# Joining 256-column projections into 512-column products with tokens on the partitions

## The chip, the cores and the metric

The kernel runs on one core of a Trainium2 chip. The metric is the device time of one execution in microseconds; "before" is the median of three executions on the chip. A profile is one further execution, recorded by the hardware profiler.

## What is computed

One block of a hybrid encoder for 256 tokens of width 2048, everything in float32. The input is normalised (u), one projection `w_in` gives the inputs of two mixers, and their outputs go through `w_out`; a SwiGLU FFN and a last normalisation follow. Cut to what the change touches:

```python
u = rms_norm(h, norm1_g[l])
P = u @ w_in[l]
z, xbc, dt_raw, pr = P[..., :o1], P[..., o1:o2], P[..., o2:o3], P[..., o3:]
prev = jnp.pad(pr, ((0, 0), (1, 0), (0, 0)))[:, :-1]
pr = pr + (prev - pr) * rwkv_mu[l]                 # token shift; r, k, v are slices of pr
xbc = jax.nn.silu(causal_depthwise_conv(xbc, conv_w, conv_b))   # x, B, C are slices of xbc
y_ssd = ssd_mixer(...)                             # chunked state space mixer, 4 groups
y_rwkv = rwkv7_mixer(...)                          # 32 heads, recurrence over the tokens
h = h + jnp.concatenate([y_ssd, y_rwkv], axis=-1) @ w_out[l]
v = rms_norm(h, norm2_g[l])
h = h + (jax.nn.silu(v @ w_gate[l]) * (v @ w_up[l])) @ w_down[l]
return rms_norm(h, norm_f_g)
```

## The kernel before

**Products in three parts.** Every large product is done in float32 accuracy with three matmuls: each operand is split into a rounded part and a rest (`uh`, `ul` for the activations, `whi`, `wlo` for the weights), and hi x hi, hi x lo and lo x hi are summed. The weights arrive by DMAs of SyncE's queue (SP) in units of 128 x 1024 elements in a ring of four `raw` buffers; ScalarE writes `whi` (L192), VectorE `wlo` (L193), each in a ring of four.

**Two forms of a product.** `gemm_a` (L267) makes 256 output columns with the weights stationary: 96 matmuls whose moving side is the 256 tokens. The result has channels on the partitions and tokens along the row. As the normalisation factor belongs to a token, VectorE multiplies the result in PSUM by a broadcast row `R` (`scaled`, L229). `gemm_b` (L284) makes 512 output columns with the activations stationary: 96 matmuls of 512 columns; the result has tokens on the partitions, so the factor can be a per-partition scale. Both keep their results in the pool `mm` of four PSUM tiles; `gemm_a` uses one tile, `gemm_b` two. A second PSUM pool, `mx`, also of four, serves all the small work.

**The order of the work.** A `Side` object holds small functions with due times. `gemm_a` advances its clock by half a tick after every two of its 16 k tiles (four ticks a product), `gemm_b` by half a tick after every k tile (eight ticks for 16). Functions whose time has come are traced there, between the product's matmuls; `drain` traces all that is left. This order is the priority by which the instructions are then laid out on each engine.

**RWKV.** There are eight pairs of two 128-channel blocks. Window `pi` (loop at L908) multiplies k, v and r of pair `pi`, 256 columns each, with the token shift (`shift`, L359: one ScalarE and one VectorE instruction a block) behind each product. From window 4 on, two output products of four k tiles (`out_rwkv`, L900) follow the values. So windows 0 to 3 have 12 ticks, windows 4 to 7 have 16. In them, `window` (L882) places three stages of side work: `PREP` for pair `pi`, `AMATS` and `INV` (the matrices and their inverse) for pair `pi - 1`, and `CHAIN` (four state steps, group norm, `final` with the output parts `yh`, `yl`) for pair `pi - 2`. With 16 ticks or more, the times hold as written, with 12 they are compressed.

**State space mixer.** After window 7, `window(8, 20)` and two output products, four 256-column products give B and C with their convolution (`conv`, L928: one ScalarE and three VectorE instructions a block) and one silu over all of `BC`. Then, for each of four groups, two 256-column products give x, convolved at once; output products of finished work and the 512-column product for z follow, with the previous group's side work (`SSD` times) in their ticks.

The FFN (L1116) uses 512-column products throughout; its gated values are turned by eight PE transposes (`back`, L1103), which are due 1.5 ticks after the up product.

Of the kernel before, what the change touches and what calls it, by code (L numbers as in the profile page):

```python
# [10 lines left out]
F32 = mybir.dt.float32  # L11
F32R = mybir.dt.float32r
AF = mybir.ActivationFunctionType
# [3 lines left out]
P = 128  # L17
T = 256
D = 2048
KT = D // P  # L20
D_FF = 5632
CXBC = 2048
CDT = 5120
CR = 5152
CK = 7200
CV = 9248
# [4 lines left out]

PREP = (1.081, 1.2, 4.2, 5.2, 5.536, 6.756, 8.05, 9.2)
AMATS = (0.132, 1.4, 2.027, 2.231, 2.69, 3.323, 6.493)
INV = (4.9, 5.9, 6.9, 8.4, 10.4, 11.4, 12.9, 14.9)
STEPS = (0.667, 2.0, 5.0)
# [31 lines left out]
def tile_hybrid_block(ctx: ExitStack, tc: tile.TileContext, x, norm1_g, w_in, conv_w, conv_b, dt_bias, A_log, D_skip,  # L69
                      ssd_norm_g, mu, w0, w2, a0, a2, g2, k_k, k_a, r_k, gn_w, gn_b, w_out, norm2_g, w_gate, w_up,  # L70
                      w_down, norm_f_g, out):
    nc = tc.nc
    PS = bass.MemoryType.PSUM
    x = x[0]
    out = out[0]
    w_in, conv_w, w2, a2, g2 = w_in[0], conv_w[0], w2[0], a2[0], g2[0]
# [4 lines left out]
    wpool = ctx.enter_context(tc.tile_pool(name="wpool", bufs=3))  # L81
# [4 lines left out]
    side = Side()  # L86
# [4 lines left out]
    def mxt(name):  # L91
        return mx.tile([P, 512], F32, name=name, tag="mx")
# [7 lines left out]
    ident = const.tile([P, P], F32, name="ident")  # L100
# [13 lines left out]
    ps = mxt("ps_up")  # L114
# [9 lines left out]
    rows = [init.tile([P, P], F32, name=f"rows{i}") for i in range(3)]  # L124
# [13 lines left out]
    MU, W0, A0, KK, KA, RK = 0, 48, 64, 80, 96, 112  # L138
# [13 lines left out]
    for hh in range(2):  # L152
        for s in range(2):
            m = mask2[hh * 64:(hh + 1) * 64, s]
# [4 lines left out]
    for s in range(2):  # L159
        for hh in range(2):  # L160
            a = hh * 64
# [20 lines left out]
    ps = mxt("ps_cols")  # L182
    nc.tensor.transpose(out=ps[:, :16], in_=rown, identity=ident[:16, :16])
    tc.keep_in_program_order(nc.vector.tensor_copy(colN, ps[:, :16]))
    colA = const.tile([P, P], F32, name="colA")
# [10 lines left out]
    uh = ul = R = None  # L196
    ssq = [const.tile([P, 2, 4], F32, name=f"ssq{i}") for i in range(3)]
    rstd = [const.tile([P, 2], F32, name=f"rstd{i}") for i in range(3)]
# [30 lines left out]
    def scaled(ps):  # L229

        nc.vector.tensor_tensor(ps, ps, R.unsqueeze(1).broadcast_to([P, 2, T]), ALU.mult)
        return ps
# [34 lines left out]
    def gemm_a(w, cols, name, units=None):  # L267
        ps = mmt(name)
        for k0 in range(0, KT, 4):
            hi, lo = split(load_a(w, cols, k0)) if units is None else units(k0 // 4)  # L270
            for k in range(4):
                kt = k0 + k
                first, last = kt == 0, kt == KT - 1
                for b in range(2):
                    o = ps[:, b]
                    wh, wl = hi[:, k, b * P:(b + 1) * P], lo[:, k, b * P:(b + 1) * P]
                    nc.tensor.matmul(o, wh, uh[:, kt], start=first and b == 0, stop=False)  # L277
                    nc.tensor.matmul(o, wh, ul[:, kt], start=False, stop=False)  # L278
                    nc.tensor.matmul(o, wl, uh[:, kt], start=False, stop=last and b == 1)  # L279
                if k % 2:  # L280
                    side.tick(0.5)
        return ps

    def gemm_b(w, r0, c0, acts, name, turned=False):  # L284


        ps = [mmt(name).rearrange("p a t -> p (a t)") for _ in range(2)]
        n = len(acts)
        wv = w[r0:r0 + n * P, c0:c0 + 512].rearrange("(k p) c -> p k c", p=P)
        for k0 in range(0, n, 2):  # L290
            raw = wpool.tile([P, 2, 512], F32, name="raw", tag="raw", bufs=4)
            if turned:
                nc.sync.dma_start(out=raw[:, 0], in_=wv[:, k0])
                for a in range(2):
                    nc.sync.dma_start(out=raw[a * 64:a * 64 + 64, 1], in_=wv[64 - a * 64:P - a * 64, k0 + 1])
            else:
                nc.sync.dma_start(out=raw, in_=wv[:, k0:k0 + 2])
            hi, lo = split(raw)
            for k in range(2):
                kt = k0 + k  # L300
                first, last = kt == 0, kt == n - 1
                ah, al = acts[kt]
                for b in range(2):
                    s = slice(b * P, (b + 1) * P)
                    nc.tensor.matmul(ps[b], ah[:, s], hi[:, k], start=first, stop=False)  # L305
                    nc.tensor.matmul(ps[b], ah[:, s], lo[:, k], start=False, stop=False)  # L306
                    nc.tensor.matmul(ps[b], al[:, s], hi[:, k], start=False, stop=last)  # L307
                side.tick(0.5)
        return ps

    def add_out(w, r0, ys, then=None, turned=False, ns=range(4)):

# [30 lines left out]
    for r, c in ((rows[1], colB), (rows[0], colA), (rows[2], colC)):  # L343
        ps = mxt("ps_cols")
# [4 lines left out]
    omA = const.tile([P, 48], F32, name="omA")  # L349
# [9 lines left out]
    def shift(dst, ps, om, m):  # L359
        nc.scalar.activation(dst, ps, AF.Copy, scale=om)  # L360
        nc.vector.scalar_tensor_tensor(dst[:, 1:], ps[:, :T - 1], m, dst[:, 1:], ALU.mult, ALU.add)
# [10 lines left out]
    pst = ExitStack()  # L372
    pp = pst.enter_context(tc.tile_pool(name="pp", bufs=1, side="right"))
# [508 lines left out]
    def window(pi, ticks):  # L882
        if pi < 8:
            w = pairs[pi]
            w["load"]()
            for t, n in zip(PREP, ("decay", "rate", "keys", "keys2", "keysum", "btt", "vt", "ktt")):
                side.at(t, w[n])
        if 0 < pi < 9:
            w = pairs[pi - 1]
            for t, f in zip(AMATS, w["amats"]):  # L890
                side.at(t, f)
            for t, f in zip(INV, w["inv"]):
                side.at(t if ticks >= 16 else t * (ticks - 0.5) / 16, f)
        if pi > 1:
            for t, f in zip(CHAIN, pairs[pi - 2]["chain"]):
                side.at(t if ticks >= 16 else t * (ticks - 0.5) / 16, f)
# [3 lines left out]
    def out_rwkv(q, ns):  # L900

        if q < 0:
            return
        if ns[0] == 0:
            held[:] = [yq.popleft(), yq.popleft()]
        add_out(w_out, 2048 + q * 512, held, turned=True, ns=ns)

    for pi in range(8):  # L908
        st = {}
        pairs.append(rwkv_pair(pi, st))  # L910
        window(pi, 16 if pi > 3 else 12)
        for i, (n, c) in enumerate((("k", CK), ("v", CV), ("r", CR))):
            ps = scaled(gemm_a(w_in, [(0, 256, c + pi * 256)], "ps_rkv"))
            t = pp.tile([P, 2, T], F32, name="rkv", tag="t" + n, bufs=1)
            for j in range(2):
                m = ((c - CR) // P) + 2 * pi + j
                shift(t[:, j], ps[:, j], omA[:, m:m + 1], colA[:, MU + m:MU + m + 1])
            st[n] = t
            if n == "v":
                out_rwkv(pi // 2 - 2, (2 * (pi % 2), 2 * (pi % 2) + 1))  # L920
        side.drain()


# [4 lines left out]
    def conv(dst, ps, blk):  # L928
        w = [colC[:, 24 * j + blk:24 * j + blk + 1] for j in range(4)]
        nc.scalar.activation(dst, ps, AF.Identity, bias=colB[:, CB + blk:CB + blk + 1], scale=w[3])  # L930
        for s in range(1, 4):
            nc.vector.scalar_tensor_tensor(dst[:, s:], ps[:, :T - s], w[3 - s], dst[:, s:], ALU.mult, ALU.add)

    for i in range(4):
        ps = scaled(gemm_a(w_in, [(0, 256, CXBC + 2048 + i * 256)], "ps_bc"))
        if i == 0:
            pst.close()
            bcp = xzst.enter_context(tc.tile_pool(name="bcp", bufs=1, side="right"))
            xz = xzst.enter_context(tc.tile_pool(name="xz", bufs=2, side="right"))
            BC = bcp.tile([P, 2, 4, T], F32, name="BC")  # L940
        for j in range(2):
            b = 2 * i + j
            conv(BC[:, b // 4, b % 4], ps[:, j], 16 + b)
    nc.scalar.activation(BC, BC, AF.Silu)
    side.drain()
    window(9, 18)

    def ssd_group(g, xc, zs):
        st = {}
# [104 lines left out]
    for g in range(4):  # L1054
        xc = []
        if g == 0:
            out_rwkv(2, (2, 3))
        elif g == 1:
            out_rwkv(3, (0, 1, 2, 3))
        for i in range(2):  # L1060
            ps = scaled(gemm_a(w_in, [(0, 256, CXBC + g * 512 + i * 256)], "ps_xs"))
            t = xz.tile([P, 2, T], F32, name="xc", tag=f"xc{i}")
            for j in range(2):
                conv(t[:, j], ps[:, j], 4 * g + 2 * i + j)
            nc.scalar.activation(t, t, AF.Silu)
            xc.append(t)
        if g >= 2:
            add_out(w_out, (g - 2) * 512, [yq.popleft() for _ in range(2)])
        psz = gemm_b(w_in, 0, g * 512, uacts, "ps_z")
        zs = xz.tile([P, 2, 512], F32, name="zs")  # L1070
        for b in range(2):
            nc.scalar.activation(zs[:, b], psz[b], AF.Silu, scale=rstd[0][:, b:b + 1])
        side.drain()
        if g == 0:
            est.close()
            est = ExitStack()
            sp = est.enter_context(tc.tile_pool(name="sp", bufs=1))
        for t, f in zip(SSD, ssd_group(g, xc, zs)):
            side.at(t if g < 3 else t / 3, f)
# [119 lines left out]
```

## Time and profile before

| | |
|---|---|
| Median of 3 executions | 1674.48 us (1671.82 to 1675.09) |
| Profiled execution | 1671.13 us |
| Its span | 1669.4 us, mean clock of TensorE 0.996 |
| DMA traffic | 286.97 MB, mean 172 GB/s |

The stages of the profiled execution, by the first matmuls of the products:

| Stage | us from the span's start |
|---|---|
| RWKV windows 0, 1, 2, 3 | 38.1, 76.6, 117.8, 185.9 |
| RWKV windows 4, 5, 6, 7 | 242.2, 309.0, 376.5, 443.7 |
| Two output products, B and C | 510.6 |
| State space groups and their output products | 585.8 |
| FFN | 930.6 to the end |

In the profile's lines, "L279 PE MATMUL ps_rkv<-uh,wlo" is a matmul of TensorE made by line 279 that writes the tile `ps_rkv`. PEld are the weight loads of TensorE, which overlap its matmuls; DVE is VectorE, ACT ScalarE, SPq the queue that issues DMAs. A line of groups ends with the busy time in us, the mean length of one in ns, and the engine's idle time before them with what ended it. Records of matmuls overlap, since they are pipelined: the time of a product is read from first start to first start.

### The profile page before, as it was taken

How to read it: one execution, taken by the hardware profiler on the slowest of the kernel's cores; microseconds unless marked ns; L12 is line 12 of the kernel's file. 1: busy time of each engine (PE TensorE's matmuls, PEld its weight loads, DVE VectorE, ACT ScalarE, POOL GpSimd, SP SyncE). 2: the span in 40 equal slices, each digit the busy share in tenths (PEclk: the TensorE clock that was granted, in tenths of full speed). 3: DMA queues.
4: the chain of work that ended last, by engine and by line, in shares of the span. 5: the costliest groups of instructions: out<-in, count | busy, mean ns of one | idle time of the engine just before them, and what ended most of it. 6: DMA issues, size and time to landing. Idle time of an engine off the chain costs nothing.

```text
span 1669.4 us, 31147 instructions
## 1 busy us (share of the span) xinstructions
PE 1640.1 (98%) x12514; PEld 1422.7 (85%) x12514; DVE 1172.9 (70%) x1827; ACT 910.7 (55%) x1488; POOL 17.9 (1%) x57
## 2 busy tenths in 40 slices
PE   8999999999999999999999999999999999999997
PEld 8998898988888988998988888888888888888886
DVE  7887898788887867877778656465565564554657
ACT  6654775766755648657665544444444444444444
POOL 3000000000000000000000000000000000000000
PEclk9998999999999999999999999999999999999999
DMA  8653554454455556765655666666666666666663
GB/s 247 184 143 104 134 135 126 137 140 139 138 142 144 154 152 188 233 191 155 180 176 152 202 189 190 194 189 189 196 190 189 190 189 196 189 191 192 190 189 126
DMA packets 219473, 286.97 MB, mean 172 GB/s; under 512 B 41762, under 2 KB 124480, under 8 KB 218688
## 3 DMA queue, kind: packets, MB, share of 16 engines
q1 hardware_dynamic: 218000, 282.68, 58.1%
q8 instruction: 98, 1.61, 0.4%
q0 software_dynamic: 752, 1.24, 0.3%
q10 hardware_dynamic: 576, 1.05, 0.2%
q14 instruction: 47, 0.39, 0.1%
HBM read 281.75 MB, written 3.18 MB: 171 GB/s over the span
## 4 chain that ended last, share of the span: by engine, by line
PE 77%; DVE 9%; ACT 6%; issue 3%; DMA 3%; SPq 1%; DVEq 0%; POOL 0%; ACTq 0%
PE ps_o L305 8%; PE ps_o L306 8%; PE ps_o L307 8%; PE ps_gt L306 5%; PE ps_up L307 5%; PE ps_gt L305 5%; PE ps_up L306 5%; PE ps_gt L307 5%; PE ps_up L305 5%; DVE wlo L193 2%; PE ps_xs L277 2%; ACT whi L192 2%; PE ps_rkv L277 2%; PE ps_xs L278 2%; PE ps_xs L279 2%
## 5 line engine op out<-in xcount | busy, mean ns | idle before, releaser
L193 DVE TENSOR_TENSOR wlo<-raw,whi 128x1024 fp32r<-128x1024 f32 x508 | 619.9, 1222 | 376.9 <-ACT whi L192 375.8
L192 ACT CAST whi<-raw 128x1024 fp32r<-128x1024 f32 x508 | 532.7, 1051 | 596.8 <-PE ps_o L307 159.6
L277 PE MATMUL ps_rkv<-uh,whi 128*128 128x256 f32 x768 | 227.7, 296 | 0.0
L279 PE MATMUL ps_rkv<-uh,wlo 128*128 128x256 f32 x768 | 218.9, 285 | 0.0
L278 PE MATMUL ps_rkv<-ul,whi 128*128 128x256 f32 x768 | 218.8, 285 | 0.0
L277 PEld LDWEIGHTS ps_rkv<-uh,whi 128*128 128x128 f32 x768 | 147.5, 192 | 5.3 <-issue 0.7
L278 PEld LDWEIGHTS ps_rkv<-ul,whi 128*128 128x128 f32 x768 | 147.9, 193 | 1.2 <-issue 0.3
L279 PEld LDWEIGHTS ps_rkv<-uh,wlo 128*128 128x128 f32 x768 | 147.6, 192 | 0.4
L305 PE MATMUL ps_gt<-whi,uh 128*128 128x512 f32 x352 | 137.1, 389 | 0.0
L307 PE MATMUL ps_gt<-whi,ul 128*128 128x512 f32 x352 | 137.0, 389 | 0.0
L306 PE MATMUL ps_gt<-wlo,uh 128*128 128x512 f32 x352 | 136.9, 389 | 0.0
L305 PE MATMUL ps_up<-whi,uh 128*128 128x512 f32 x352 | 136.9, 389 | 0.0
L306 PE MATMUL ps_up<-wlo,uh 128*128 128x512 f32 x352 | 136.9, 389 | 0.0
L307 PE MATMUL ps_up<-whi,ul 128*128 128x512 f32 x352 | 136.9, 389 | 0.0
L305 PE MATMUL ps_o<-whi,ah 128*128 128x512 f32 x336 | 131.7, 392 | 0.0
L307 PE MATMUL ps_o<-whi,al 128*128 128x512 f32 x336 | 130.9, 390 | 0.0
L306 PE MATMUL ps_o<-wlo,ah 128*128 128x512 f32 x336 | 130.7, 389 | 0.0
L305 PE MATMUL ps_o<-whi,yh 128*128 128x512 f32 x256 | 105.6, 412 | 0.0
L307 PE MATMUL ps_o<-whi,yl 128*128 128x512 f32 x256 | 100.9, 394 | 0.0
L306 PE MATMUL ps_o<-wlo,yh 128*128 128x512 f32 x256 | 100.8, 394 | 0.0
L318 DVE TENSOR_TENSOR h<-ps_o,h 128x512 f32<-128x512 f32 x152 | 98.5, 682 | 1.7 <-PE ps_o L307 1.1
L306 PEld LDWEIGHTS ps_up<-wlo,uh 128*128 128x128 f32 x352 | 66.1, 188 | 13.7
(342 smaller groups left out, 2982.4 us busy)
## 6 DMA issues: line engine op xcount, KB each, us to landing
raw<-in_w_in_dram SPq DMA_DIRECT2D x180, 512.0 KB, 4.0
raw<-in_w_gate_dram SPq DMA_DIRECT2D x88, 512.0 KB, 3.7
raw<-in_w_up_dram SPq DMA_DIRECT2D x88, 512.0 KB, 3.7
raw<-in_w_down_dram SPq DMA_DIRECT2D x88, 512.0 KB, 4.6
raw<-in_w_out_dram SPq DMA_DIRECT2D x32, 512.0 KB, 4.0
raw<-in_w_out_dram SPq DMA_DIRECT2D x32, 256.0 KB, 4.2
raw<-in_w_out_dram SPq DMA_DIRECT2D x64, 128.0 KB, 4.0
csb<-cs_d SPq DMA_DIRECT2D x4, 1024.0 KB, 6.5
```

What stands on the lines that cost most here:

```text
L192: order(nc.scalar.copy(hi, raw))
L193: order(nc.vector.tensor_tensor(lo, raw, hi.bitcast(F32), ALU.subtract))
L277: nc.tensor.matmul(o, wh, uh[:, kt], start=first and b == 0, stop=False)
L278: nc.tensor.matmul(o, wh, ul[:, kt], start=False, stop=False)
L279: nc.tensor.matmul(o, wl, uh[:, kt], start=False, stop=last and b == 1)
L305: nc.tensor.matmul(ps[b], ah[:, s], hi[:, k], start=first, stop=False)
L306: nc.tensor.matmul(ps[b], ah[:, s], lo[:, k], start=False, stop=False)
L307: nc.tensor.matmul(ps[b], al[:, s], hi[:, k], start=False, stop=last)
L318: nc.vector.tensor_tensor(d, ps[b], d, ALU.add)
```

## The change

Thirteen pairs of 256-column products become 512-column products through a new function `rows_of`:

- the values of pair `pi` with the keys of pair `pi + 1` (`pi` 0 to 6), from two ranges of weight columns, which `gemm_b` now takes as a tuple and loads by two DMAs a unit; the keys of pair 0 get a product of their own ahead of window 0, and the values of pair 7 keep theirs in window 7
- B, and C
- x of each of the four groups

`rows_of` copies the two PSUM tiles to SBUF on ScalarE with the token's factor as scale, into a tile of the `raw` ring, and returns a function that turns 256 channels by four PE transposes into one `mx` tile. Token shifts and convolutions read that tile; they are side work now, due one tick after the product (1.5 for the second half of x). The silu over `BC` is done in two halves. The receptance r stays as it was. Two due times in `PREP` change: `vt` from 8.05 to 9.6, `ktt` from 9.2 to 8.05.

```diff
-PREP = (1.081, 1.2, 4.2, 5.2, 5.536, 6.756, 8.05, 9.2)
+PREP = (1.081, 1.2, 4.2, 5.2, 5.536, 6.756, 9.6, 8.05)
...
-        wv = w[r0:r0 + n * P, c0:c0 + 512].rearrange("(k p) c -> p k c", p=P)
+        parts = [(0, 256, c0[0]), (256, 256, c0[1])] if isinstance(c0, tuple) else [(0, 512, c0)]
+        wv = w[r0:r0 + n * P].rearrange("(k p) c -> p k c", p=P)
...
-                nc.sync.dma_start(out=raw, in_=wv[:, k0:k0 + 2])
+                for at, m, c in parts:
+                    nc.sync.dma_start(out=raw[:, :, at:at + m], in_=wv[:, k0:k0 + 2, c:c + m])
...
+    def rows_of(c0, name):
+
+
+        ps = gemm_b(w_in, 0, c0, [(uh[:, k], ul[:, k]) for k in range(KT)], name)
+        rows = wpool.tile([P, 2, 512], F32, name="rows_in", tag="raw", bufs=4)
+        for b in range(2):
+            nc.scalar.activation(rows[:, b], ps[b], AF.Copy, scale=rstd[0][:, b:b + 1])
+
+        def channels(i):
+            ps = mxt("ps_tr").rearrange("p (j t) -> p j t", j=2)
+            for j in range(2):
+                for b in range(2):
+                    c = i * 256 + j * P
+                    nc.tensor.transpose(out=ps[:, j, b * P:(b + 1) * P], in_=rows[:, b, c:c + P], identity=ident)
+            return ps
+
+        return channels
...
+    def channels_of(st, n, pi, ps):
+        t = pp.tile([P, 2, T], F32, name="rkv", tag="t" + n, bufs=1)
+        for j in range(2):
+            m = (dict(k=CK, v=CV, r=CR)[n] - CR) // P + 2 * pi + j
+            shift(t[:, j], ps[:, j], omA[:, m:m + 1], colA[:, MU + m:MU + m + 1])
+        st[n] = t
+
+    sts = [{} for _ in range(8)]
+    channels_of(sts[0], "k", 0, scaled(gemm_a(w_in, [(0, 256, CK)], "ps_rkv")))
     for pi in range(8):
-        st = {}
+        st = sts[pi]
         pairs.append(rwkv_pair(pi, st))
         window(pi, 16 if pi > 3 else 12)
...
+        if pi < 7:
+
+            turn_to = rows_of((CV + pi * 256, CK + (pi + 1) * 256), "ps_vk")
+            side.at(1, lambda f=turn_to, st=st, pi=pi: channels_of(st, "v", pi, f(0)))
+            side.at(1, lambda f=turn_to, st=sts[pi + 1], pi=pi: channels_of(st, "k", pi + 1, f(1)))
+        else:
+            channels_of(st, "v", pi, scaled(gemm_a(w_in, [(0, 256, CV + pi * 256)], "ps_rkv")))
+        out_rwkv(pi // 2 - 2, (2 * (pi % 2), 2 * (pi % 2) + 1))
+        channels_of(st, "r", pi, scaled(gemm_a(w_in, [(0, 256, CR + pi * 256)], "ps_rkv")))
         side.drain()
...
-        ps = scaled(gemm_a(w_in, [(0, 256, CXBC + 2048 + i * 256)], "ps_bc"))
...
-    nc.scalar.activation(BC, BC, AF.Silu)
+    def conv_bc(f, i):
+        for m in range(2):
+            ps = f(m)
+            for j in range(2):
+                b = 2 * m + j
+                conv(BC[:, i, b], ps[:, j], 16 + 4 * i + b)
+        nc.scalar.activation(BC[:, i], BC[:, i], AF.Silu)
+
+    turn_b = rows_of(CXBC + 2048, "ps_bc")
...
+    side.at(1, lambda: conv_bc(turn_b, 0))
+    turn_c = rows_of(CXBC + 2560, "ps_bc")
     side.drain()
     window(9, 18)
+    side.at(1, lambda: conv_bc(turn_c, 1))
...
-        for i in range(2):
-            ps = scaled(gemm_a(w_in, [(0, 256, CXBC + g * 512 + i * 256)], "ps_xs"))
+        turn_x = rows_of(CXBC + g * 512, "ps_xs")
+
+        def conv_x(i, f=turn_x, g=g, xc=xc):
             t = xz.tile([P, 2, T], F32, name="xc", tag=f"xc{i}")
+            ps = f(i)
             for j in range(2):
                 conv(t[:, j], ps[:, j], 4 * g + 2 * i + j)
             nc.scalar.activation(t, t, AF.Silu)
             xc.append(t)
+
+        side.at(1, lambda f=conv_x: f(0))
+        side.at(1.5, lambda f=conv_x: f(1))
```

More of the change, by code (lines that the diff above doesn't have):

```diff
@@ L292, in gemm_b @@
             if turned:
-                nc.sync.dma_start(out=raw[:, 0], in_=wv[:, k0])
+                nc.sync.dma_start(out=raw[:, 0], in_=wv[:, k0, c0:c0 + 512])
                 for a in range(2):
-                    nc.sync.dma_start(out=raw[a * 64:a * 64 + 64, 1], in_=wv[64 - a * 64:P - a * 64, k0 + 1])
-            else:
-                nc.sync.dma_start(out=raw, in_=wv[:, k0:k0 + 2])
+                    nc.sync.dma_start(out=raw[a * 64:a * 64 + 64, 1],
+                                      in_=wv[64 - a * 64:P - a * 64, k0 + 1, c0:c0 + 512])
+            else:
+                for at, m, c in parts:
+                    nc.sync.dma_start(out=raw[:, :, at:at + m], in_=wv[:, k0:k0 + 2, c:c + m])
             hi, lo = split(raw)
@@ L906, in out_rwkv @@
         add_out(w_out, 2048 + q * 512, held, turned=True, ns=ns)
+    def channels_of(st, n, pi, ps):
[6 more added lines that the diff above has]
+    channels_of(sts[0], "k", 0, scaled(gemm_a(w_in, [(0, 256, CK)], "ps_rkv")))
     for pi in range(8):
-        st = {}
+        st = sts[pi]
         pairs.append(rwkv_pair(pi, st))
         window(pi, 16 if pi > 3 else 12)
[L912 to L920, printed above, removed]
+        if pi < 7:
[6 more added lines that the diff above has]
+        channels_of(st, "r", pi, scaled(gemm_a(w_in, [(0, 256, CR + pi * 256)], "ps_rkv")))
         side.drain()
@@ L932, in conv @@
             nc.vector.scalar_tensor_tensor(dst[:, s:], ps[:, :T - s], w[3 - s], dst[:, s:], ALU.mult, ALU.add)
-    for i in range(4):
-        ps = scaled(gemm_a(w_in, [(0, 256, CXBC + 2048 + i * 256)], "ps_bc"))
[L936 to L943, printed above, removed]
-    nc.scalar.activation(BC, BC, AF.Silu)
+    def conv_bc(f, i):
[6 more added lines that the diff above has]
+    turn_b = rows_of(CXBC + 2048, "ps_bc")
+    pst.close()
+    bcp = xzst.enter_context(tc.tile_pool(name="bcp", bufs=1, side="right"))
+    xz = xzst.enter_context(tc.tile_pool(name="xz", bufs=2, side="right"))
+    BC = bcp.tile([P, 2, 4, T], F32, name="BC")
+    side.at(1, lambda: conv_bc(turn_b, 0))
+    turn_c = rows_of(CXBC + 2560, "ps_bc")
     side.drain()
     window(9, 18)
+    side.at(1, lambda: conv_bc(turn_c, 1))
     def ssd_group(g, xc, zs):
```

## The prediction

> **What bounds the kernel now.** I read the page's busy shares first, then the granted clock in 40 slices, then busy time stage by stage.
>
> ```profile
> PE 1640.1 (98%) x12514; PEld 1422.7 (85%) x12514; DVE 1172.9 (70%) x1827; ACT 910.7 (55%) x1488; POOL 17.9 (1%) x57
> PEclk9998999999999999999999999999999999999999
> ```
>
> TensorE is busy for 98% of the span; the clock dips once, in the fourth slice. A share over the whole span hides stages, so next the windows by stage:
>
> ```profile
> 76.50:117.80 41.30, 41.10 (x383) 39.90 (x383) 35.76 (x65) 24.51 (x41) 0.12 (x1) 1.00 0.50 136
> 117.80:185.80 68.00, 62.59 (x998) 57.16 (x996) 53.95 (x109) 39.51 (x98) 1.00 (x5) 0.92 0.47 123
> 376.50:443.60 67.10, 65.39 (x854) 58.56 (x853) 57.46 (x111) 44.91 (x103) 0.56 (x3) 1.00 0.51 140
> 443.60:510.60 67.00, 65.55 (x856) 58.74 (x855) 57.72 (x111) 45.07 (x103) 0.56 (x3) 1.00 0.49 137
> 510.60:585.70 75.10, 74.37 (x942) 68.58 (x941) 62.18 (x117) 38.91 (x86) 0.00 (x0) 1.00 0.55 157
> 727.30:801.60 74.30, 74.30 (x443) 65.47 (x442) 55.73 (x89) 48.49 (x64) 0.00 (x0) 1.00 0.58 170
> ```
>
> Columns: stretch and length, then PE, its weight loads, VectorE, ScalarE, POOL, clock, DMA share, GB/s. The rows are windows 1, 2, 6 and 7 of the RWKV pairs, the stage of B and C, and one state space group. TensorE fills 97.5% to 100% of every one but window 2; VectorE reaches 86% (57.46 of 67.10), so it is second. The changed stages pay for TensorE time, and for stops of TensorE. Window 2 has the one long stop:
>
> ```profile
> 117.80:123.20 5.40, 5.40 (x46) 5.22 (x44) 5.40 (x7) 4.35 (x8) 0.44 (x2) 1.00 0.81 203
> 123.20:125.47 2.27, 0.03 (x1) 0.03 (x1) 1.46 (x5) 0.00 (x0) 0.00 (x0) 1.00 1.03 209
> 125.47:135.70 10.23, 9.61 (x184) 8.85 (x184) 6.41 (x11) 1.07 (x2) 0.12 (x1) 0.50 0.46 128
> 125.47 0.75 PE L712 MATMUL ps_b<-X,atb 32*32 32x32 f32 x21 [2.25 <-DVE X L701]
> ```
>
> TensorE waits 2.25 us for X, the inverse chain of pair 0 behind a VectorE busy 5.40 us of 5.40, and then runs 10.23 us at half clock. As half of those 10.23 us is lost at most, the stop costs up to 2.25 + 5.1 = 7.4 us. The Trainium skill ("TensorE: Matmul & The Clock Gate", "HAM oscillation") lets the clock fall after idle gaps over about 3.4 us; here a shorter gap was enough, and the measurement decides. By the page a stop of this length would cost 2.25 us alone.
>
> **The products.** Two 256-column products become one of 512 columns, 13 times (7 of values with keys, 2 of B and C, 4 of x). I took one product of each kind without side work in it:
>
> ```profile
> 65.04:76.56 11.52, 11.52 (x99) 11.52 (x97) 1.65 (x3) 0.94 (x2) 1.00 0.69 187
> 1064.02:1085.78 21.76, 21.76 (x96) 17.83 (x95) 0.29 (x1) 1.00 0.58 191
> ```
>
> The first is a 256-column product with the weights stationary: 96 matmuls (three neighbours overlap the window) in 11.52 us, 120 ns each, although one matmul's record is some 290 ns long: they are pipelined, so only the pace counts. The second is a 512-column product with the tokens stationary: 96 matmuls in 21.76 us, 226.7 ns each. Twice 120 is 240, so a matmul has a constant part of 240 - 226.7 = 13.3 ns, and 96 matmuls fewer save 2 x 11.52 - 21.76 = 1.28 us. That is all the wide form brings: no pass over the data is saved.
>
> The Trainium skill ("TensorE: Matmul & The Clock Gate", "Back-to-back issue gap") gives N/2.4 + 2.5 ns warm: 109.2 ns at 256 and 215.8 ns at 512 columns. By that a product would save an estimated 192 x 109.2 - 96 x 215.8 ns = 0.25 us, not 1.28; the trace does not agree (120 and 226.7 ns).
>
> **The transposes.** Each product adds eight of 128 x 128. The nearest are the FFN's eight, between 512-column matmuls:
>
> ```profile
> 1089.63 0.39 PE L307 MATMUL ps_o<-whi,al 128*128 128x512 f32 x1
> 1089.86 1.03 PE L1109 MATMUL ps_t<-ident,gt 128*128 128x128 f32 x8
> 1090.65 0.48 PE L305 MATMUL ps_o<-whi,ah 128*128 128x512 f32 x1
> 1090.97 0.40 PE L306 MATMUL ps_o<-wlo,ah 128*128 128x512 f32 x1
> ```
>
> From 1089.63 to 1090.97 are 1.34 us in which two matmuls would have taken 0.45: eight transposes cost 0.89 us. Each product keeps 1.28 - 0.89 = 0.39 us, and 13 of them 5.1 us. That is the sure term.
>
> **The other engines.**
>
> ```profile
> L231 DVE TENSOR_TENSOR ps_rkv<-ps_rkv,R 128x512 f32<-128x512 f32 x24 | 16.7, 694 | 9.1 <-PE ps_rkv L279 9.1
> L1072 ACT ACTIVATE zs<-ps_z,rstd 128x512 f32<-128x512 f32 x8 | 5.2, 686 | 1.0 <-PE ps_z L307 1.0
> L192 ACT CAST whi<-raw 128x1024 fp32r<-128x1024 f32 x508 | 532.7, 1051 | 596.8 <-PE ps_o L307 159.6 <-PE ps_up L307 140.0 <-PE ps_gt L307 123.9
> raw<-in_w_in_dram SPq DMA_DIRECT2D x180, 512.0 KB, 4.0
> ```
>
> VectorE loses 26 scalings, 26 x 0.694 = 18 us; ScalarE gains 26 copies with a scale, priced by the silu of z at 0.686 us, 18 us also. Neither engine sets the end where TensorE is at 97.5% or more, so both count nothing; without that cover VectorE's part would be a gain of 1.4 us a window. Splits, token shifts, convolutions and their numbers stay. The copies stand in ScalarE's queue ahead of the next products' splits; whoever waits for those is TensorE, but the splits themselves wait longest for TensorE (the row of L192), so they run ahead and 1.4 us is covered. One unit is 2.7 us of TensorE (12 matmuls by 226.7 ns); if that lead is gone, each copy costs its length.
>
> The row tile sits in one of the four raw weight buffers until its transposes are done. SP's queue may then wait for that buffer, and the loads and side transfers behind it with it: a load lands in 4.0 us and three buffers hold 8 us of work, so I take nothing, and 2.7 us a product if the split's lead is used up. The value and key products issue 16 loads of 256 KB instead of 8 of 512 KB; the trace shows no such product, but the r, k and v loads already have the same 1 KB rows. I take nothing; SP only issues. The second silu over B and C may reload a table on ScalarE, beside TensorE's work: nothing. The swap of the vt and ktt turns only follows the values' later arrival.
>
> **A new wait.** The transposes need both copies, and everything behind them on TensorE's queue waits too. They are placed one tick, 2.7 to 2.9 us of matmuls, after the product; the copies take 1.4 us if ScalarE is free at once, so 1.3 us of room. Bounds: the FFN's transposes wait for nothing worth noting (1.4 us before 88 of their weight loads), and the sum over keys waits in the windows:
>
> ```profile
> L1109 PEld LDWEIGHTS ps_t<-ident,gt 128*128 128x128 f32 x88 | 10.3, 140 | 1.4
> L557 PE MATMUL ps_sum<-red,sel 128*128 128x16 f32 x32 | 4.6, 256 | 2.0 <-DVE red L539 1.6 <-ACT kp L516 0.4
> ```
>
> The second has 2.0 us over 8 pairs, 0.25 us each. I take 0.1 us, 1.3 us in all; the ends are 0 and a copy late by 1 us, 13 us.
>
> **The shifted key product.** Pair 0's keys move ahead of window 0, so the 11.52 us of window 7's key product leave it: 12 ticks remain, while its side work is laid out for up to 14.9 and the rest is drained at the end. TensorE gets to the next output product, which needs the final yl of pair 5, that much earlier. Before, it fits exactly:
>
> ```profile
> 487.14 0.30 PE L814 MATMUL ps_y<-sn,ar 64*64 64x64 f32 x8
> 510.59 0.40 PE L305 MATMUL ps_o<-whi,yh 128*128 128x512 f32 x1
> 513.66 0.69 DVE L868 TENSOR_TENSOR yl<-yc,yh 128x512 fp32r<-128x512 f32 x1
> 514.40 0.19 PEld L307 LDWEIGHTS ps_o<-whi,yl 128*128 128x128 f32 x1 [0.40 <-DVE yl L868]
> 521.57 0.51 PE L557 MATMUL ps_sum<-red,sel 128*128 128x16 f32 x4
> ```
>
> The last state step (tick 9.9) is at 43.5 us of the window, yl is ready 27.2 us later, at 70.8 (514.35 - 443.6), and TensorE waited 0.40 us for it. After, tick 10 comes at about the same 43 us, but the window's TensorE work ends at 67.0 - 11.5 = 55.5 us. Ready then are the pair 4 halves of two output products, 24 matmuls or 5.4 us: 60.9. Pair 7's sums follow the r product by 11 us (510.6 to 521.6) and bring some 5 us of side work: 65.9. So the wait lies between 0 (the chain is 5 us shorter, with fewer splits beside it) and 9.9 us (70.8 - 60.9, no side work ready). I take 2.5 us. At the front the moved product gives nothing back: TensorE was full there (41.10 of 41.30).
>
> **Sum.** -5.1 + 1.3 + 2.5 = -1.3 us. The profiled execution took 1671.1 us (span 1669.4), 3.3 below the median of 1674.5; I set the difference against the median: 1673.2.
>
> **Rivals.**
> 1. *Nothing is given back.* Copies always early, yl in time: -5.1, 1669.4 us. For it: ScalarE is busy 55%. Against: the 0.40 us wait shows that yl has no room. Chance 0.18.
> 2. *The stop at 123 us goes too.* Two scalings fewer ahead of X in window 1 spare 1.4 us of 2.25 on a VectorE that was full; the 0.40 us wait of TensorE shown above ran on at clock 1.00 (row 510.60). -1.3 - 7.4 gives 1665.8. Against: the instructions' order is worked out anew, and window 1 is shorter by 0.4 us. Chance 0.20.
> 3. *Slower: TensorE stands still for yl of pair 5.* It decides when yl is over 2.3 us later than TensorE's other work, since that long a stop halved the clock. Price at the far end: 9.9 + 5.1 us at half clock; 1674.5 - 5.1 + 1.3 + 15 = 1685.7. Chance 0.14.
> 4. *Slower: the copies are late at every product*, 1 us each: 1674.5 - 5.1 + 2.5 + 13 = 1684.9. For it: in the windows ScalarE runs bursts and waits of several us. Chance 0.10.
> 5. *The constant part of a matmul vanishes in this form*, as the skill's formula has it: 0.25 - 0.89 = -0.64 us a product, so 8.3 us slower plus 3.8: 1686.6. Both paces were read in this trace, on the same engine and types, so 0.02.
>
> **How the numbers follow.** My forecast, a saving mostly given back (1671 to 1677), gets 0.36. About 0.2%, 3.3 us, is what a measurement of this kernel can tell from no change. Faster: rivals 1 and 2, 0.38. Same: 0.36. Slower: rivals 3 to 5, 0.26. Cases of both signs hold most of the chance; the range of 1664 to 1685 leaves out the tails below rival 2 and above rival 4.
>
> **What would show it.** Right: the 512-column products at 227 ns a matmul, 0.9 us for eight transposes, windows 4 to 6 shorter by 0.2 to 0.5 us each, VectorE's total 18 us lower, ScalarE's 18 higher. Wrong: idle time of TensorE's loads before the new transposes named after the copies (rival 4); a gap over 2.3 us near window 7's end and a clock of 0.5 behind it (rival 3); no dip in the fourth slice (rival 2); windows shorter by over 1 us, which would mean VectorE had been the bound.

## The result

| | Median, us | Ratio to before |
|---|---|---|
| Before, on the same chip | 1673.15 (1668.65 to 1675.09, 4 executions) | |
| Changed kernel | 1753.34 (1749.45 to 1755.17, 4 executions) | 1.0479, 95% interval 1.0456 to 1.0502 |

The change makes the kernel 4.8% slower, some 80 us. The prediction said 1673.2 us, with a range from 1664 to 1685. Each run of this document was set against the kernel before on its own chip, where that took a median of 1668.4 to 1673.2 us. So runs of different chips are compared by their ratios, or by the lengths of single stages in their profiles.

The page of the changed kernel answers to the first rows shown of before: busy time of each engine, then the granted clock in 40 slices.

```profile
PE 1672.6 (96%) x11370; PEld 1380.1 (79%) x11370; DVE 1164.8 (67%) x1801; ACT 920.0 (53%) x1511; POOL 17.7 (1%) x57
PEclk9999999899999999999999999999999999999999
```

The slices hide it: TensorE is still at 96%, and only one slice of the clock shows an 8. The stages show more. These are the windows by stage of the changed kernel, with the columns of the prediction's (stretch and length; busy time of PE, its weight loads, VectorE, ScalarE, POOL; clock; DMA share; GB/s). They are RWKV windows 1, 2, 6 and 7, the stage of B and C, and one state space group.

```profile
95.55:147.42 51.87, 46.78 (x478) 40.07 (x477) 39.95 (x71) 25.88 (x44) 0.56 (x3) 0.90 0.46 130
147.42:211.20 63.78, 58.52 (x726) 47.63 (x725) 50.88 (x100) 40.81 (x101) 0.55 (x3) 0.95 0.37 100
422.49:497.69 75.20, 68.67 (x766) 56.10 (x765) 58.79 (x109) 46.35 (x105) 0.56 (x3) 0.95 0.47 126
497.69:550.76 53.07, 50.60 (x686) 44.53 (x685) 46.07 (x90) 31.22 (x71) 0.56 (x3) 1.00 0.54 148
550.76:643.64 92.88, 85.37 (x907) 64.87 (x905) 62.65 (x127) 50.14 (x116) 0.00 (x0) 0.96 0.40 113
797.54:876.64 79.10, 76.04 (x354) 62.03 (x353) 54.24 (x87) 46.93 (x64) 0.00 (x0) 0.98 0.52 159
```

The stages with a 512-column product are longer: window 6 by 8.1 us (75.20 for 67.10), the state space group by 4.8 (79.10 for 74.30). Window 2 alone is shorter (63.78 for 68.00), since the kernel before had its long stop and its one long stretch at half clock there. In each of these stages TensorE is idle for 3 to 8 us, and the clock is below 1.00. Window 7, which lost its key product and has no wide one, is 13.9 us shorter, 11.5 of which is that product. The FFN, untouched, is equal. So the loss is spread over the stages rather than sitting in one place.

The weight loads' waits of the changed kernel (engine, tile and line, what ended the wait; total us, how often, the longest) name what is late:

```profile
PEld ps_w L801 <- ACT rs L791: 15.3, 6, 3.7
PEld ps_o L308 <- ACT whi L192: 10.9, 7, 3.7
PEld ps_rkv L277 <- ACT whi L192: 10.7, 4, 3.1
PEld ps_tr L327 <- ACT rows_in L320: 4.9, 9, 1.4
PEld ps_z L308 <- ACT whi L192: 3.0, 2, 2.7
```

All five are ScalarE's work. Three of them, 24.6 us, are waits for first weight splits (`whi`), nearly all in the product that follows a wide one: one such wait, of 0.3 to 3.7 us, stands behind each of the 13. The new transposes' own wait (`ps_tr` for the row tile) is only 4.9 us. In the kernel before none of TensorE's groups has a first split among what ended its waits.

The largest, 15.3 us for `rs`, a copy of the state steps, comes for 11.1 us from the ends of the wide products in windows 4 to 6. The first of these three stops, ScalarE and then TensorE (start, us, engine, line, what; in brackets the idle time before it and what ended it):

```profile
309.88 1.27 ACT L320 ACTIVATE rows_in<-ps_vk,rstd 128x512 f32<-128x512 f32 x2
...
312.84 0.33 ACT L791 COPY rs<-ps_r 128x64 f32<-128x64 f32 x2
```

```profile
313.11 0.60 PE L801 MATMUL ps_w<-rs,XF 64*64 64x64 f32 x8 [3.56 <-ACT rs L791]
```

The row copies, and four copies of `ktt` behind them, stand ahead of `rs` in ScalarE's queue. Nor could the next product fill the stop, since its first split comes only at 316.01.

### One wide product, followed

I took the x product that starts at 876.64 us. First its TensorE rows and then ScalarE's timeline, in the changed kernel:

```profile
901.52 0.39 PE L310 MATMUL ps_xs<-whi,ul 128*128 128x512 f32 x1
901.75 1.02 PE L1049 MATMUL ps_st<-xs,btok 128*128 128x512 f32 x2
905.66 0.80 PE L308 MATMUL ps_o<-whi,yh 128*128 128x512 f32 x1 [2.89 <-ACT whi L192]
```

```profile
889.27 1.05 ACT L192 CAST whi<-raw 128x1024 fp32r<-128x1024 f32 x1 [0.64 <-ACT btok L1013]
901.32 1.31 ACT L320 ACTIVATE rows_in<-ps_xs,rstd 128x512 f32<-128x512 f32 x2 [10.99 <-PE ps_xs L310]
902.53 1.05 ACT L1022 ACTIVATE L<-L 128x1024 f32<-128x1024 f32 x1
...
904.57 1.04 ACT L192 CAST whi<-raw 128x1024 fp32r<-128x1024 f32 x1
```

ScalarE makes the last split of the x product at 889.27 and then stands idle for 10.99 us, until the x product ends and its rows can be copied. Only behind the copies, at 904.57, comes the first split of the next product, so TensorE waits. Was the data missing? The loads of the next product in that time (issues of line 300, and their time to landing):

```profile
L300 SPq DMA_DIRECT2D raw<-in_w_out_dram x3: 367/368/368, 885.5 to 891.7; - x3
...
DMA to landing us min/median/max: 3.6/3.6/3.7
```

The three loads landed between 889.1 and 895.4, 6 to 12 us before the copies. So ScalarE was free and the weights were there, and it did not split them: the copies stand ahead of those splits in its queue. The same reading of the other twelve wide products: from the start of the last split before the copies to that of the copies are 9.1 to 19.4 us, at all 13. (In the others ScalarE has other work in that time, but no split.)

The stops cost a second time through the clock:

```profile
902.20:905.60 3.40, 0.56 (x2) 0.00 (x0) 0.00 (x0) 3.40 (x6) 0.00 (x0) 0.95 0.01 2
905.60:912.00 6.40, 6.30 (x16) 4.51 (x17) 4.24 (x5) 3.47 (x5) 0.00 (x0) 0.50 0.44 140
```

After 3.4 us in which TensorE is busy for 0.56 us, the next 6.4 us run at clock 0.50. The mean clock over the whole span:

```profile
core 0: 1750.3 us, clock 0.976
```

It was 0.996 before. A clock of 0.976 over 1750.3 us is at most 42 us of lost full-speed time, against 6.7 before (0.004 x 1669.4), so up to 35 of the 80 us are the clock. The rest is idle time of TensorE, which grew by 48 us (span less busy time: 77.7 us, 29.3 before).

### The profile page after: what moved, and what is told of

Its sections match the earlier page's. It is cut to its first block, busy times and chain, and to the rows that moved or that the text cites. A ratio compares the mean times of both kernels' runs of the same rounds, so it can differ in the third digit from the quotient of the medians.

```text
span 1750.3 us, 28931 instructions
## 1 busy us (share of the span) xinstructions
PE 1672.6 (96%) x11370; PEld 1380.1 (79%) x11370; DVE 1164.8 (67%) x1801; ACT 920.0 (53%) x1511; POOL 17.7 (1%) x57
## 3 DMA queue, kind: packets, MB, share of 16 engines
q10 hardware_dynamic: 576, 1.05, 0.2%
## 4 chain that ended last, share of the span: by engine, by line
PE 76%; ACT 8%; DVE 8%; DMA 5%; issue 2%; SPq 1%; DVEq 0%; POOL 0%; ACTq 0%
PE ps_o L308 7%; PE ps_o L309 7%; PE ps_o L310 7%; PE ps_gt L310 5%; PE ps_up L308 5%; PE ps_gt L308 5%; PE ps_up L310 5%; PE ps_gt L309 5%; PE ps_up L309 5%; DVE wlo L193 2%; PE ps_z L309 2%; DMA raw<-in_w_in_dram 2%; ACT whi L192 2%; PE ps_z L310 2%; PE ps_vk L308 2%
## 5 line engine op out<-in xcount | busy, mean ns | idle before, releaser
L192 ACT CAST whi<-raw 128x1024 fp32r<-128x1024 f32 x508 | 532.1, 1051 | 562.4 <-PE ps_o L310 160.3
L277 PE MATMUL ps_rkv<-uh,whi 128*128 128x256 f32 x320 | 97.4, 304 | 9.4 <-ACT whi L192 9.4
L279 PE MATMUL ps_rkv<-uh,wlo 128*128 128x256 f32 x320 | 94.8, 296 | 2.1 <-DVE wlo L193 2.1
L308 PE MATMUL ps_vk<-whi,uh 128*128 128x512 f32 x224 | 94.3, 421 | 0.0
L278 PE MATMUL ps_rkv<-ul,whi 128*128 128x256 f32 x320 | 93.5, 292 | 0.0
L309 PE MATMUL ps_vk<-wlo,uh 128*128 128x512 f32 x224 | 88.1, 393 | 0.0
L310 PE MATMUL ps_vk<-whi,ul 128*128 128x512 f32 x224 | 88.1, 393 | 0.0
L310 PEld LDWEIGHTS ps_up<-whi,ul 128*128 128x128 f32 x352 | 66.1, 188 | 13.8
```

Of the source, the lines that this page charges most:

```text
L192: order(nc.scalar.copy(hi, raw))
```

## Experiments

**Theory A.** `rows_of` takes its row tile from the `raw` ring (L318), which otherwise only holds loaded weights. The tile is written late, when its product ends. In the order in which the instructions were laid out on ScalarE, all splits of later ring tiles stand behind that writing. Rival **B**: the wide product with its copies and transposes is late in itself, wherever the row tile lies. Rival **C**: the ring simply has one buffer fewer for weights.

### e1: the row tiles outside the ring

```diff
-        rows = wpool.tile([P, 2, 512], F32, name="rows_in", tag="raw", bufs=4)
+        rows = tiles()
...
+        return [pp.tile([P, 2, T], F32, name="rows_in", tag="t" + n, bufs=1) for n in "vk"]
...
+        return [xz.tile([P, 2, T], F32, name="rows_in", tag=f"xc{i}") for i in range(2)]
```

The values, keys and B use the first pair of tiles, C and x the second: two halves of 256 channels, so four copies instead of two.

> The changed kernel with the row tiles taken out of the raw weight ring: for values and keys they use the buffers of the tiles that the token shift writes anyway, for C and x those of xc; everything else of the change stays. Theory A (the row tile's place in the ring puts all weight splits of the next product behind the copies on ScalarE, so TensorE finds no weights at each of the 13 product ends): the stops after the products and nearly all half-clock time go; 1673 + 13 for the wait at the end of window 7 - 5 for the shorter products = 1681 us, between 1670 and 1690. Theory B (the later arrival of v and k and the bursts of transposes, shifts and convolutions lengthen the side work's chains): still 1735 to 1755 us. Theory C (the clock alone: more half-clock phases because TensorE pauses at the transposes): still over 1720 us.

Measured: 1694.00 us, ratio 1.0125 (1.0093 to 1.0157). Some 59 of the 80 us are gone by moving the row tile. (That its copies are four instead of two is not the reason: e8 below has four copies and the loss.) The same x product in e1, ScalarE and then the weight loads:

```profile
844.57 1.05 ACT L192 CAST whi<-raw 128x1024 fp32r<-128x1024 f32 x1 [1.67 <-PE ps_xs L310]
847.25 1.04 ACT L192 CAST whi<-raw 128x1024 fp32r<-128x1024 f32 x1 [1.62 <-PE ps_xs L310]
851.12 1.57 ACT L321 ACTIVATE rows_in<-ps_xs,rstd 128x256 f32<-128x256 f32 x4 [2.83 <-PE ps_xs L310]
852.56 1.07 ACT L192 CAST whi<-raw 128x1024 fp32r<-128x1024 f32 x1
```

```profile
851.15 0.19 PEld L310 LDWEIGHTS ps_xs<-whi,ul 128*128 128x128 f32 x1
851.38 0.19 PEld L308 LDWEIGHTS ps_o<-whi,yh 128*128 128x128 f32 x1
```

Splits of the next product now run ahead of the copies, the last of them 3.9 us before, and the next product's weight loads follow the x product's last by 0.23 us. So in the changed kernel it was not a missing buffer for the splits' results that held them up either: at this point of the product e1, with the same ring of four, finds one. Over all 13 products the last split stands 1.0 to 6.9 us before the copies, where it was 9.1 to 19.4. The clock comes back with it:

```profile
core 0: 1693.3 us, clock 0.991
```

That is at most 15 us of lost clock instead of 42. Rival B is out as the main cause. But 1694 is above A's own range in the expectation (1670 to 1690): something else is left, which e5 to e7 look for. In the undisturbed state space group the wide x product does bring what was worked out for it:

```profile
752.50:826.50 74.00, 74.00 (x354) 61.41 (x353) 54.00 (x87) 47.51 (x66) 0.00 (x0) 1.00 0.56 171
```

74.00 us at 74.00 busy and full clock, for 74.30 before: 0.3 us less, where 0.39 was forecast.

### e2: a ring tile in the kernel before

```diff
+    def ring_tile(ps):
+        d = wpool.tile([P, 2, 512], F32, name="extra", tag="raw", bufs=4)
+        for b in range(2):
+            nc.scalar.copy(d[:, b, 0:T], ps[:, b])
```

It is called behind 13 products of the kernel before: the values of pairs 0 to 6, every second product of B and C, the second x product of each group. Nothing reads the tile.

> The kernel before, with nothing of the change but this: after 13 of its 256-column products (values of pairs 0 to 6, two of B and C, the second of each x) ScalarE also copies the result into a tile of the raw ring that nobody reads. Theory A: slower by 40 to 70 us, 1713 to 1743, with ScalarE idle before the copies and TensorE waiting for whi after these products. Theories B and C: 13 x 0.9 us more ScalarE work that lies beside TensorE, so 1673 to 1678 us.

Measured: 1751.57 us, ratio 1.0466 (1.0428 to 1.0505). No wide product, no transpose, and a loss of the same size is there, more than the 40 to 70 us that theory A gave it. ScalarE and TensorE of e2 around a value product:

```profile
115.91 0.65 ACT L288 COPY extra<-ps_rkv 128x256 f32<-128x256 f32 x2 [3.96 <-DVE ps_rkv L231]
...
118.36 1.04 ACT L192 CAST whi<-raw 128x1024 fp32r<-128x1024 f32 x1
```

```profile
119.45 0.58 PE L277 MATMUL ps_rkv<-uh,whi 128*128 128x256 f32 x1 [4.90 <-ACT whi L192]
```

The picture is that of the changed kernel: the last split long before the copies (12.4 to 20.1 us at all 13), then 4.9 us of TensorE waiting for the first split. The sum agrees with the changed kernel's by more than the places do: e2 also stops TensorE for 6.1 us in each of two state space groups, where y is transposed, which the changed kernel does not. So e2 shows that a late-written tile in this ring is enough for a loss of this size, not that each microsecond is the same one.

### e3 and e4: a ring of three

e4 is the kernel before, e3 the changed kernel with a row tile of its own; both have three `raw` buffers, so that the tile of its own takes the memory of the fourth.

```diff
-            raw = wpool.tile([P, 2, 512], F32, name="raw", tag="raw", bufs=4)
+            raw = wpool.tile([P, 2, 512], F32, name="raw", tag="raw", bufs=3)
...
-        rows = wpool.tile([P, 2, 512], F32, name="rows_in", tag="raw", bufs=4)
+        rows = wpool.tile([P, 2, 512], F32, name="rows_in", bufs=1)
```

> The kernel before with three raw buffers instead of four, as a control for the run with a row tile of its own: if a load less in flight is covered, within 5 us of 1673; if the number of buffers is what the change lost, 1700 us or more.

> The changed kernel with a row tile of its own and three raw buffers instead of four (the same memory). Theory A: like the row tiles outside the ring of four, plus what a shorter ring costs, 1675 to 1700 us. Theory B: 1735 to 1755. If it is the smaller number of raw buffers that hurts and not the order, this run stays above 1735 as well.

Measured: e4 1694.95 us, ratio 1.0129 (1.0082 to 1.0177); e3 1695.86 us, 1.0135 (1.0088 to 1.0182). e4 lies between the two cases of its expectation. A buffer less for the whole execution costs 22 us, so rival C should cost less than that, since the row tile holds its buffer only part of the time. With three buffers on both sides the change costs 0.9 us, inside the intervals. So a buffer missing and the tile's place in the ring are two things, and the second is the larger one. That e3 is no slower than e1 (1.0135 and 1.0125), so that the 21 us left in e1 and the price of a shorter ring don't add, no run explains.

### e8: only the x products' rows in the ring

```diff
+        if tiles is None:
+            ring = wpool.tile([P, 2, 512], F32, name="rows_in", tag="raw", bufs=4)
+            rows = [ring[:, :, i * 256:(i + 1) * 256] for i in range(2)]
...
-        turn_x = rows_of(CXBC + g * 512, "ps_xs", own_rows)
+        turn_x = rows_of(CXBC + g * 512, "ps_xs", None)
```

> Row tiles outside the ring for values, keys, B and C, but in the ring for the four x products. The ring's price was (1753 - 1694) / 13 = 4.5 us a product; if each pays it alone, 1694 + 18 = 1712 us, with the loss in the four stretches behind the x products. If the loss came from the number of such tiles close together in the windows, 1694 to 1698.

Measured: 1713.62 us, ratio 1.0271 (1.0244 to 1.0297). The chip was another than e1's. By the ratios e8 is 24 us over e1, with some 7 us of uncertainty; in the profiles the state space groups, with the four x products, are 20.8 us longer (369.9 for 349.2), 5.2 us for each ring tile. Thirteen of them would be 68; from e1 to the changed kernel are 59. The groups of e8 show the same waiters again:

```profile
L308 PE MATMUL ps_o<-whi,yh 128*128 128x512 f32 x256 | 108.4, 426 | 6.3 <-ACT whi L192 6.3
L308 PE MATMUL ps_z<-whi,uh 128*128 128x512 f32 x128 | 50.1, 398 | 2.3 <-ACT whi L192 2.3
```

### Where e1's other 21 us are

In the profiled executions the difference is 24 us (spans of 1693.3 and 1669.4). First starts of the products in the profiled executions, as lengths of stages (us):

| Stage | Before | Changed | e1 |
|---|---|---|---|
| to the first of them | 38.1 | 39.9 | 39.8 |
| windows 0, 1 (with the moved key product, 11.5) | 79.7 | 107.6 | 92.3 |
| windows 2, 3 | 124.4 | 125.6 | 119.9 |
| windows 4, 5, 6 | 201.5 | 224.7 | 209.9 |
| window 7 | 66.9 | 53.1 | 55.6 |
| two output products, B, C | 75.2 | 92.9 | 88.4 |
| state space groups | 344.9 | 368.3 | 349.2 |
| FFN | 738.8 | 738.4 | 738.3 |

e1 loses 13.2 us with the two output products, B and C, 8.4 in windows 4 to 6, 4.3 in the state space groups, and gains 4.5 in windows 2 and 3, where the old stop for X is shorter (1.66 us between two starts of TensorE's matmuls, for 2.52) and leaves the clock at 1.00.

### e5: the product of B ahead of the two output products

```diff
     window(8, 20)
-    out_rwkv(2, (0, 1))
...
     side.at(1, lambda: conv_bc(turn_b, 0))
+    out_rwkv(2, (0, 1))
```

This is e1 with other work for TensorE where it waited for pair 5. First e1 at that place, its timeline and its windows (stretches of time):

```profile
531.21 0.68 DVE L562 TENSOR_REDUCE red<-tmp 128x16 f32<-128x512 f32 x1
532.00 0.50 PEld L580 LDWEIGHTS ps_sum<-red,sel 128*128 128x128 f32 x2 [4.65 <-issue]
...
532.93 0.69 DVE L891 TENSOR_TENSOR yl<-yc,yh 128x512 fp32r<-128x512 f32 x1
533.67 0.29 PEld L310 LDWEIGHTS ps_o<-whi,yl 128*128 128x128 f32 x1 [0.32 <-DVE yl L891]
```

```profile
517.45:545.40 27.95, 23.62 (x263) 17.58 (x261) 21.34 (x43) 15.72 (x39) 0.00 (x0) 0.88 0.40 111
...
527.40:529.80 2.40, 0.38 (x2) 0.00 (x0) 2.40 (x4) 2.32 (x5) 0.00 (x0) 1.00 0.12 29
529.80:536.60 6.80, 4.57 (x20) 3.65 (x21) 5.09 (x11) 1.76 (x5) 0.00 (x0) 0.50 0.62 164
```

The two output products take 27.95 us from start to start, 16.7 before. TensorE stands still first for pair 7's sums (its loads for 4.65 us; their `red` is behind a VectorE busy 2.40 of 2.40 us), then for `yl`, 0.32 us. 6.8 us at half clock follow.

> Row tiles outside the ring, and the product for B, which needs only the input, stands ahead of the two output products after window 7 instead of behind them. If the 11 us lost there (28.0 us for the two output products against 16.7 before) are TensorE's wait for yl and the sums of pairs 5 and 7, the stage from window 7's end to the state space groups gets shorter by 8 to 12 us: 1682 to 1686. If the loss is side work that must be done there anyway, no change: 1694 +- 3.

Measured: 1683.22 us, ratio 1.0098 (1.0067 to 1.0130); the interval is wide, since the executions spread from 1680.55 to 1692.49. The place itself, in e5's windows:

```profile
512.20:590.80 78.60, 77.97 (x830) 60.60 (x829) 61.04 (x119) 50.65 (x112) 0.00 (x0) 1.00 0.46 136
```

78.60 us instead of 88.4, TensorE full and no half clock: the stop is gone by giving TensorE other work there. 3.4 us over before's 75.2 are left. The stage is shorter by 9.8 us, as expected; e9, with the same order, repeats it (79.1 us), while e3, e6 and e8, without it, have 84.9 to 86.5. The whole time shows it less clearly. Of the 10.8 us between the medians of e1 and e5, 4.2 are the chip (the kernel before took 1672.5 us on e1's and 1668.4 on e5's); by the ratios e5 is 4.5 us under e1, and the intervals overlap.

### e6 and e7: the copies on VectorE; only B, C and x wide

e6 is e1 with this edit; e7 is e1 with the values and keys as in the kernel before, so that 6 of the 13 products are wide.

```diff
-                nc.scalar.activation(rows[i][:, b], ps[b][:, i * 256:(i + 1) * 256], AF.Copy,
-                                     scale=rstd[0][:, b:b + 1])
+                nc.vector.tensor_scalar(rows[i][:, b], ps[b][:, i * 256:(i + 1) * 256], rstd[0][:, b:b + 1], None,
+                                        ALU.mult)
```

> Row tiles outside the ring, copied by VectorE instead of ScalarE. If the 2 to 4 us that windows 4 to 6 lose come from the copies' burst on ScalarE ahead of the step's copy rs, they go: 1694 - 8 = 1686 us. If the windows lose them by the order of the transposes and shifts, no change; and as VectorE has 18 us more work, the rival that VectorE is the bound in the windows gives 1700 or more.

> Only B, C and x in the new form, row tiles outside the ring; values and keys as before the change, so no key product is moved. Theory: the end of window 7 and the RWKV windows are as before, six products save 0.39 us each, and the stage of B, C and the first group keeps its loss of up to 6 us: 1671 to 1679 us. If the values and keys are not where the remaining 21 us come from, 1685 to 1695.

Measured: e6 1684.64 us, ratio 1.0101 (1.0085 to 1.0116); e7 1674.95 us, ratio 1.0034 (1.0020 to 1.0049). Two groups of TensorE's waits tell where the windows lose, first e1, then e6, then e7 (the last part is the idle time and what ended it):

```profile
L803 PE MATMUL ps_w<-rs,XF 64*64 64x64 f32 x256 | 12.9, 245 | 6.8 <-ACT rs L793 6.8
...
L580 PE MATMUL ps_sum<-red,sel 128*128 128x16 f32 x32 | 5.2, 270 | 10.8 <-DVE red L562 8.9 <-ACT whi L192 2.0
```

```profile
L803 PE MATMUL ps_w<-rs,XF 64*64 64x64 f32 x256 | 13.0, 244 | 1.7 <-ACT rs L793 1.6
...
L580 PE MATMUL ps_sum<-red,sel 128*128 128x16 f32 x32 | 5.1, 268 | 13.9 <-DVE red L562 12.4 <-ACT pr L517 1.5
```

```profile
L803 PE MATMUL ps_w<-rs,XF 64*64 64x64 f32 x256 | 12.3, 241 | 1.9 <-ACT rs L793 1.9
...
L580 PE MATMUL ps_sum<-red,sel 128*128 128x16 f32 x32 | 4.5, 253 | 2.0 <-DVE red L562 1.6 <-ACT kp L539 0.4
```

With the copies on ScalarE the state steps wait for `rs` (6.8 us); with them on VectorE that goes (1.7), but the sums over keys wait longer for `red` (13.9 for 10.8). Windows 4 to 6 stay long: 208.1 us in e6, for 209.9 in e1 and 201.5 before. So the windows did not get back the 8 us of e6's expectation, though 1684.64 looks like it: e6 ran on the faster chip, its ratio is only 4 us under e1's, and the intervals overlap. The waits mostly move from one engine's queue to the other's. With the values and keys narrow both waits are what they were before (1.9 and 2.0), and windows 4 to 6 too (201.1 us). What e7 still loses is in the state space groups (349.3 us, e1 349.2, before 344.9). So the windows' loss belongs to the wide value and key products; whether to the copies, to the later token shifts or to the new order alone was not separated.

### e9 and e10: the remedies together

e9 is e5 with e6's edit, e10 is e7 with it.

> The changed kernel with the rows outside the ring of raw weights, the product of B ahead of two output products (as in e5), and the copies of the rows on VectorE instead of ScalarE (as in e6); the whole computation is done. If the two remedies act on different places, they add: e1 (1694.0) less e5's 10.8 and e6's 9.4 gives about 1674, which is within 0.4% of the kernel before on this chip (ratio 0.998 to 1.006). If both removed the same stretches at half clock, or VectorE is full at the windows' ends, only the larger gain stays: 1680 to 1684, ratio 1.007 to 1.010. Below the kernel before by more than 0.2% only if the saving of 5.1 us that was forecast comes through in full.

> Only B, C and x as 512-column products (6 of the 13), rows outside the ring of raw weights, values and keys as before, and the copies of the rows on VectorE instead of ScalarE; the whole computation is done. e7, the same with the copies on ScalarE, gave ratio 1.0034. If what is left there is splits late behind the copies on ScalarE, the ratio falls to 0.998 to 1.001 (six products save 6 x 0.39 = 2.3 us less one stretch at half clock of 3.4 us at 642). If VectorE's rest splits are what is late (the trace of e7 names wlo for two gaps), the copies on VectorE make these later, and the ratio stays at 1.003 to 1.006.

Measured: e9 1681.74 us, ratio 1.0048 (1.0031 to 1.0065); e10 1674.42 us, ratio 1.0004 (0.9988 to 1.0020). The 10.8 and 9.4 us that e9's expectation takes off compare e1 with runs on a faster chip; by the ratios they are 4.5 and 4.0. Taken off e1's 1.0125 they give 1.0074, so e9 at 1.0048 shows no sign that the two remedies take away the same stretches. Its windows 4 to 6 still take 208.5 us. e10 is near the first case of its expectation: the two waits of TensorE for `wlo` in e7, of 1.05 and 2.59 us, are gone with the copies on VectorE, and the state space groups take 347.5 us for 349.3. But it cannot be told from the kernel before: no version with wide products was faster than it. The 2.3 us that six of them should save (6 x 0.39) did not show.

## Why the prediction was wrong

Point by point, in the prediction's own order:

- **The products, 1.28 us less, and the transposes, 0.89 us more: right in size.** In the changed kernel the matmuls of the wide products start 227 to 229 ns apart in the median (226.7 forecast). Where nothing stops, a group with one wide x product is 0.3 us shorter (e1's 74.00). That gain is small beside any stop.
- **The splits of the next product, "so they run ahead and 1.4 us is covered": wrong, and with it the step that failed, the row tile in one of the four raw weight buffers, where "I take nothing".** I asked whether the buffers would hold enough loaded weights, and they did: the loads landed 6 us and more before the copies. I did not ask what a tile of this ring, written only at the end of its product, does to the order of ScalarE's queue. The row read for the lead, L192's, is a sum over the whole span of the kernel before, and of the 596.8 us of waits in it the gate and up products of the untouched FFN ended 264. The splits that ran ahead in the kernel before stand behind the copies; the lead is used up at each of the 13 products. The fallback price of 2.7 us a product was also too low: from e1 to the changed kernel are 59 us, 4.6 a product, since stops of up to 3.7 us bring stretches at half clock behind them. Which rule of the layout puts the splits there is inferred from the kernels with the tile inside and outside, not seen.
- **VectorE 18 us less, ScalarE 18 us more, nothing for the end: right in length, wrong in place.** The copies had the forecast length (0.68 us each, 17.8 in all). The page's totals moved by 8 and 9 us only, since the page counts the time of overlapping records once. The records' lengths, added up, fall by 18.6 us on VectorE and rise by 12.7 on ScalarE, where four table loads of 1.28 us fewer make up for the rest. The place was another matter: ScalarE's queue set the end at 53% busy.
- **The new wait, 0.1 us a product: too small, but inside its bounds.** The transposes' weight loads waited 4.9 us for the row tile in the changed kernel, 1.3 forecast, 13 as the far bound. That is 3.6 of the 80 us.
- **The shifted key product, 2.5 us between 0 and 9.9: the mechanism right, the term mis-sized.** Window 7's work ended 55.6 us after its start (55.5 forecast) and `yl` 71.7 us after it (70.8). But the 5 us of side work from pair 7's sums, which was to cover half of the gap, was itself late behind VectorE. So the time there was nearer the far bound, with the half clock of rival 3: 11.3 us (27.95 for 16.7). e5, which fills the gap, shows the cause.
- **Windows 4 to 6, 0.2 to 0.5 us shorter each: wrong without the ring too.** They are 8.4 us longer in e1. The terms left out were the waits for `rs` and `red`, which e7 removes; what in the wide products makes them was not separated.
- **The rivals.** Rival 4 (copies late by 1 us at every product) had the right engine and the wrong waiter: the next product's splits, not the transposes. Rival 3 came true in its place, at 11.3 of its 15 us. Rival 2 did not show in the changed kernel, and came true in part in windows 2 and 3 of e1. No rival held that a ring tile reorders the queue.

The bound of the unknown cost was the fault behind the range: the row tile's price was argued from capacity alone (8 us of work in three buffers), so its far end was never worked out over 13 products. At 2.7 us each, a price that the prediction named itself, it would have been 35 us.

## What to carry to other kernels

A tile from a ring that feeds a prefetch is a place in an order, not only memory: a tile written at the end of a product, taken from the ring of the next product's weights, can hold back the work on those weights although they have landed. Look, at such a product's end, at how long before it the prefetching engine did its last piece; a long idle time ended by the product itself is the sign. A gain of 0.4 us a product cannot pay for a lost lead, which cost some 5 us a product here, so a rewrite whose sure gain is that small is judged by its queues and not by its matmuls.

## What the runs showed of the hardware

The clock falls after shorter stops than the 2.3 us that I had assumed. The Trainium skill ("TensorE: Matmul & The Clock Gate", "HAM oscillation") names idle gaps over about 3.4 us. In e1 a stop of 1.39 us was enough, and so was the second of two stops of 1.83 us, but not the first, in these rows of its timeline, with the windows behind the first and the last:

```profile
363.56 0.45 PE L803 MATMUL ps_w<-rs,XF 64*64 64x64 f32 x8 [1.83 <-ACT rs L793]
...
433.04 0.45 PE L803 MATMUL ps_w<-rs,XF 64*64 64x64 f32 x8 [1.83 <-ACT rs L793]
...
470.88 0.59 PE L580 MATMUL ps_sum<-red,sel 128*128 128x16 f32 x4 [1.39 <-DVE red L562]
```

```profile
363.50:367.00 3.50, 3.44 (x26) 3.00 (x27) 2.75 (x4) 2.85 (x6) 0.00 (x0) 1.00 0.03 5
...
471.80:475.20 3.40, 3.40 (x17) 3.06 (x18) 1.69 (x5) 1.65 (x5) 0.00 (x0) 0.50 0.21 75
```

So the length of one gap does not decide it here. The stretches at half clock in the changed kernel's first 1012 us are all of 3.4, 6.8 or 10.2 us: 15 of them, where before had one. The clock's records in the traces show what does fit. Within each execution all stretches at half clock start whole multiples of 3.413 us apart; in e1 those at 434.26 and 471.81 us are 11 such slices apart. Counted on this grid, from 38 to 930 us in the traces of all twelve kernels, a slice at full clock in which TensorE's matmuls leave less than 1.0 us idle was never followed by half clock (2178 slices), one with 1.87 us or more always (46), and one in between in 22 of 71 cases. The first stop of 1.83 us lay across two slices, 0.86 and 0.97 us in them; the second lay in one.
